# A decoder layer on one core: the last two products of the down stage share an output and its banks, the gate's dots move to the second block's map

## Chip, cores and metric

The kernel runs on 1 core of one Trainium2 chip. Times are device microseconds of one execution; the time of a kernel is the median of its runs. Engines are TensorE (PE; its weight loads are PEld), VectorE (DVE), ScalarE (ACT), GpSimd (POOL) and SyncE (SP); in this kernel SP and POOL issue the DMAs.

## The reference

Shapes: x is 1 × 2048 × 1024, the hidden width is 4096, one layer, all in float32.

```python
mod = (cond @ w_ada[l] + b_ada[l])[:, None, :]
sh1, sc1, g1, sh2, sc2, g2 = jnp.split(mod, N_MOD, axis=-1)
...
mix = jnp.concatenate([y_conv, y_pool], axis=-1) @ w_out[l]
x = _layer_norm(DEEPNORM_ALPHA * x + (1.0 + g1) * mix, ln1_g[l], ln1_b[l])

h = x * (1.0 + sc2) + sh2
f = jnp.square(jax.nn.relu(h @ w_mlp_in[l])) @ w_mlp_out[l]
x = _layer_norm(DEEPNORM_ALPHA * x + (1.0 + g2) * f, ln2_g[l], ln2_b[l])
```

The change touches the last three lines: the two products of the MLP, the gate g2 (a row of 1024 numbers, itself a product of `cond` with a part of `w_ada`) and the last normalisation.

## The kernel before

**Precision.** Each float32 operand is cut in two: ACT makes the high part by a cast (L145), the DVE the rest by a subtraction (L146, the "split"). A product of two operands is then three matmuls (L152, L153, L154: high × high, high × low, low × high), called `mm3` here.

**Stages.** The 2048 tokens are two blocks of 1024, b = 0 and 1. For each block: input projection with the token mixing, output projection with the first normalisation, then `first_map`, which makes the hidden state and squares its positive part. When both blocks are done, `down` multiplies the hidden state by w2 and normalises. In the profiled execution the stages lie about so: block 0 to 283, its map 283 to 575, block 1's input projection 575 to 745, its output projection to 845, its map 845 to 1149, down 1149 to 1717, the rest the tail.

**Fast products.** The maps use a Strassen-like scheme of seven products of blocks (`up(b, g)` for eight column groups g; 24 matmuls for each of the seven, group by group, with weights summed on the fly). `down` uses a scheme with 26 products, the table `PRODUCTS`. A row of it is (slot of the hidden state's sums, weights with signs, sign, whether the banks start anew, reads). "Reads" are (t, d, sign): the product's four banks are added to output tile group t, column half d, `F[t, d]`. A product whose row says False goes on accumulating in the banks of the product of two rows before (there are two sets of four banks, `banks[n % 2]`). One product is four units of 24 matmuls (gp = 0 to 3), one for each quarter of the inner dimension.

**State sums.** The slots of the hidden state for `down` are sums of its blocks. `sums(stage)` in `up` makes them on the DVE, 256 columns at a time, and POOL stores them to `usum` in DRAM. The sums of weights are made by accumulating DMAs from POOL (`sums_down`, into `wsum`), one each seven `mm3` where `W_BEATS` says so: 27 in block 1's input projection and 53 in its map.

**Beside the first block's map.** `first_map` calls `beside` 48 times, from the end of group 0 to the end of group 7 (beats 0 to 47, seven a group). At each beat of the first block the iterator `first_side` may begin a job: `sum_x` and `sum_first` (four and two; they load, combine and store blocks for block 1's input projection), then the eight `gate_dot`s (load 512 KB of `w_ada`, one DVE dot) and `gate_row`, which turns the dots into the row g2: a bias on the DVE (L277, the tile `mod`), a transpose on PE (L225), a way through DRAM. A job that loads begins with its DMA and is finished three beats later. Loads of the dots are in POOL's queue.

**Order.** Each engine and each DMA queue runs its instructions in the order in which they are issued; `operand(n, gp)` is issued four units ahead of the unit that uses it. Tiles come from rings: `o` has ten tiles (128 × 1024), `r` five, `w` six, `h` 28, PSUM eight banks (`ps`). A tile that is asked for while all are in use makes the asking instruction wait for the oldest one's last user.

**The end.** `LATE` is the tile group that the last product writes. `read` adds a product's banks to F; where that was the last addition to F[t, d], `finish` multiplies by g2 and adds the residual, which `residual` made beforehand and saved (`rsave`), and `Close.normalise` does the last normalisation. The last product has banks of its own; its weights are multiplied by g2 in `operand` (`if n == last`), so that its banks can be added without a gate. The rows of LATE get their statistics by `bn_stats` on the DVE (L1340), all others by squares on ACT (`stats_act`, L835).

## Time and profile before

| | |
|---|---|
| median of 3 runs | 1734.94 us (1734.08 to 1737.56) |
| the profiled execution's own time | 1733.62 us |
| its span in the trace | 1731.8 us |
| granted TensorE clock, mean | 0.994 |
| bytes moved by DMA | 461.07 MB |

The span reaches from the first to the last instruction on the core; what lies around it is 1.8 us. The profile's rows read: start, duration, engine, line, operation, output<-inputs (buffer numbers left out), shape, count, and in brackets the idle time of that engine just before and what ended it. Busy times of matmuls overlap in their pipeline, so durations of 0.39 go with starts 0.23 apart.

### The profile page before, as it was taken

The page shows a single profiled execution, that of the slowest core. Times are in us where ns is not written, and L with a number is a line of the kernel's source. Part 1 is how long each engine was busy: PE and PEld are TensorE (multiplying, and loading weights), DVE is VectorE, ACT ScalarE, POOL GpSimd, SP SyncE. Part 2 cuts the span into 40 slices and gives each one's busy share as a digit, 9 for nine tenths or more (in the row PEclk, how much of TensorE's full clock was granted, in tenths as well). Part 3 has the DMA queues.
Part 4 walks back from the last instruction along what each step waited for, and adds up shares of the span by engine and source line. Part 5 has one row for each costly group of instructions (what it writes and reads, how often), then busy time and mean ns, then how long its engine had stood idle before and what let it go on. Part 6 is the DMA issues. An engine that isn't in the chain of part 4 may idle for free.

```text
span 1731.8 us, 21979 instructions
## 1 busy us (share of the span) xinstructions
PE 1691.5 (98%) x7519; PEld 1397.7 (81%) x7519; DVE 1394.1 (81%) x2123; ACT 840.7 (49%) x1148; POOL 382.4 (22%) x695
## 2 busy tenths in 40 slices
PE   9999999999999999999999999999999999999996
PEld 8888888787887778878878888888888888888885
DVE  8897798888888776878797777685788886598999
ACT  6323358555444843445854454464544433353542
POOL 0222221345544302220245555430000000000000
PEclk9999999999999999999999999999999999999998
DMA  9998777677674767895989999888899997678672
GB/s 387 346 341 316 302 264 252 211 225 243 229 220 162 236 210 214 208 330 185 305 250 263 262 263 259 227 279 335 309 336 346 354 344 289 198 246 296 243 272 94
DMA packets 146912, 461.07 MB, mean 266 GB/s; under 512 B 20200, under 2 KB 20720, under 8 KB 146800
## 3 DMA queue, kind: packets, MB, share of 16 engines
q1 hardware_dynamic: 89728, 290.80, 47.3%
q0 software_dynamic: 57072, 168.87, 32.3%
q8 instruction: 59, 0.97, 0.2%
q14 instruction: 53, 0.43, 0.1%
HBM read 345.81 MB, written 155.72 MB: 290 GB/s over the span
## 4 chain that ended last, share of the span: by engine, by line
PE 52%; DVE 10%; DMA 4%; issue 2%; ACT 1%; POOL 0%; DVEq 0%; SPq 0%; ACTq 0%; POOLq 0%
PE ps L154 17%; PE ps L152 17%; PE ps L153 17%; DVE o L162 2%; DVE h L146 2%; DVE w L146 1%; DVE h L162 1%; DVE o L1366 1%; DVE o L1361 1%; DMA r<-gout 1%; DMA r<-wosum 1%; DMA usum<-o 1%; DVE r L162 1%; PE ps L856 0%; DMA r<-in_w 0%
## 5 line engine op out<-in xcount | busy, mean ns | idle before, releaser
L154 PE MATMUL ps<-h,w 128*128 128x512 f32 x1312 | 511.9, 391 | 12.2 <-DVE w L146 12.2
L152 PE MATMUL ps<-h,w 128*128 128x512 f32 x1312 | 511.8, 391 | 5.0 <-ACT o L1070 3.0
L153 PE MATMUL ps<-h,w 128*128 128x512 f32 x1312 | 511.8, 390 | 0.0
L152 PE MATMUL ps<-h,h 128*128 128x512 f32 (+1 forms) x1064 | 412.5, 388 | 3.5 <-ACT o L730 1.7
L153 PE MATMUL ps<-h,h 128*128 128x512 f32 (+1 forms) x1064 | 412.3, 388 | 1.0 <-DVE h L146 1.0
L154 PE MATMUL ps<-h,h 128*128 128x512 f32 (+1 forms) x1064 | 412.4, 388 | 0.0
L154 PEld LDWEIGHTS ps<-h,w 128*128 128x128 f32 x1312 | 247.2, 188 | 66.4 <-DVE w L146 15.4
L152 PEld LDWEIGHTS ps<-h,w 128*128 128x128 f32 x1312 | 246.8, 188 | 57.6 <-ACT o L1070 3.4
L153 PEld LDWEIGHTS ps<-h,w 128*128 128x128 f32 x1312 | 247.2, 188 | 51.6
L1095 POOL DMA_DIRECT2D usum<-o x416 | 226.3, 552 | 276.6 <-DVE o L162 185.5
L145 ACT CAST w<-r 128x1024 fp32r<-128x1024 f32 x156 | 164.2, 1053 | 224.6 <-PE ps L153 200.4
L145 ACT CAST h<-r 128x1024 fp32r<-128x1024 f32 (+1 forms) x144 | 144.5, 1010 | 247.2 <-PE ps L153 80.3
L146 DVE TENSOR_TENSOR w<-r,w 128x1024 fp32r<-128x1024 f32 x156 | 189.3, 1218 | 79.1 <-ACT w L145 78.5
L152 PEld LDWEIGHTS ps<-h,h 128*128 128x128 f32 x1064 | 199.7, 188 | 45.7 <-ACT o L730 2.1
L146 DVE TENSOR_TENSOR h<-r,h 128x1024 fp32r<-128x1024 f32 (+1 forms) x144 | 167.1, 1167 | 84.9 <-ACT h L145 84.8
L153 PEld LDWEIGHTS ps<-h,h 128*128 128x128 f32 x1064 | 199.8, 188 | 42.0 <-DVE h L146 1.3
L154 PEld LDWEIGHTS ps<-h,h 128*128 128x128 f32 x1064 | 199.8, 188 | 40.9
L162 DVE TENSOR_TENSOR o<-o,o 128x256 f32<-128x256 f32 (+2 forms) x458 | 199.6, 484 | 3.7 <-DMA usum<-o 1.2
L162 DVE TENSOR_TENSOR o<-o,ps 128x512 f32<-128x512 f32 x172 | 114.4, 679 | 19.9 <-PE ps L154 19.1
L145 ACT CAST h<-w 128x1024 fp32r<-128x1024 f32 x104 | 108.7, 1046 | 41.2 <-DVE w L162 36.6
L146 DVE TENSOR_TENSOR h<-w,h 128x1024 fp32r<-128x1024 f32 x104 | 126.6, 1218 | 1.9 <-ACT h L145 1.6
L162 DVE TENSOR_TENSOR r<-r,r 128x1024 f32<-128x1024 f32 x60 | 73.3, 1221 | 33.0 <-DMA r<-in_w 29.6
(166 smaller groups left out, 1415.4 us busy)
## 6 DMA issues: line engine op xcount, KB each, us to landing
usum<-o POOLq DMA_DIRECT2D x416, 128.0 KB, 5.5
r<-usum SPq DMA_DIRECT2D x104, 512.0 KB, 5.4
w<-in_w SPq DMA_DIRECT2D x80, 512.0 KB, 6.3
w<-wsum SPq DMA_DIRECT2D x68, 512.0 KB, 6.7
r<-in_w SPq DMA_DIRECT2D x60, 512.0 KB, 6.9
wsum<-in_w POOLq DMA_DIRECT2D x56, 512.0 KB, 9.3
wsum<-wsum POOLq DMA_DIRECT2D x24, 512.0 KB, 6.2
msum<-o POOLq DMA_DIRECT2D x18, 512.0 KB, 7.0
```

The source lines that it names most:

```text
L145: high = nc.scalar.copy(hi, src)
L146: return high.ins, nc.vector.tensor_tensor(lo, src, hi.bitcast(F32), op=ALU.subtract).ins
L152: nc.tensor.matmul(ps, whi, xhi, start=first, stop=False, skip_group_check=goes_on)
L153: nc.tensor.matmul(ps, whi, xlo, start=False, stop=False, skip_group_check=goes_on)
L154: done = nc.tensor.matmul(ps, wlo, xhi, start=False, stop=last, skip_group_check=goes_on)
L162: return nc.vector.tensor_tensor(out_, a, b_, op=op)
L1095: nc.gpsimd.dma_start(usum[slot, g // 2, :, b, g % 2, :], z)
L1361: nc.vector.scalar_tensor_tensor(z[:, cs], self.F[t][:, cs], mv[:, 0:1], self.rows[0][:, cs], op0=op, op1=ALU.mult)
L1366: nc.vector.scalar_tensor_tensor(z[:, cs], z[:, cs], mv[:, 6:7], self.rows[1][:, cs], op0=ALU.mult, op1=ALU.add)
```

## The change

It has four parts.

1. *The end of the down stage.* The 26 products are the same; their order, some signs and shares of banks are new. The last two (slots 10 and 18, weights w0 and w2) go to the same output (2, 0): product 24 starts new banks and reads nothing, product 25 accumulates in them (`last_product` uses `banks[(last - 1) % 2]`). LATE is 2 now, not 1. Both weights are multiplied by g2 beforehand: `residual` becomes `prepared`, a list of 16 residual jobs and 8 weight jobs (load 512 KB, two DVE instructions, store to `wsum`, which has two places more), begun at product 1, not 3. `operand` multiplies nothing any more. `Close.tail`, the rows with bn_stats, is one row only; the other three use ACT's squares.
2. *The gate's dots* move from the first block's map to the second's (`second_side`), with their loads in SP's queue, begun at beats 4, 6, 11, 13, 18, 20, 25 and 27, the row at 31. The six sums of `first_side` begin at beats 5, 11, 13, 18, 20 and 26; before, at 0, 4, 8, 12, 16 and 20.
3. *The last group's state sums* of block 0 are owed to `flush`, which is called behind the first product of the next input projection.
4. `W_BEATS`' first range ends at 200, not 232.

```diff
@@ -28,7 +28,7 @@
-W_BEATS = {*range(48, 232, 7), *range(336, 752, 7)}
+W_BEATS = {*range(48, 200, 7), *range(336, 752, 7)}
 
@@ -63,32 +63,32 @@
 )
 PRODUCTS = (
-    (10, ((0, 1),), -1, True, ()),
+    (4, ((13, 1), (14, 1)), -1, True, ((2, 0, -1),)),
     (1, ((2, 1),), 1, True, ((0, 0, -1),)),
-    (18, ((2, 1),), 1, False, ((2, 0, -1),)),
+    (6, ((1, 1), (15, -1)), -1, False, ((2, 1, 1),)),
     (5, ((12, 1),), -1, False, ((0, 1, 1), (2, 1, 1))),
...
+    (20, ((4, 1),), 1, True, ((1, 0, 1),)),
     (14, ((3, 1),), 1, False, ((3, 1, -1),)),
-    (22, ((16, 1),), 1, False, ((0, 1, 1),)),
+    (2, ((3, 1), (15, 1)), -1, True, ((0, 1, -1),)),
     (24, ((8, 1),), 1, False, ((0, 1, -1),)),
-    (19, ((4, 1), (17, 1)), 1, False, ((0, 0, -1),)),
+    (12, ((1, 1),), 1, False, ()),
     (25, ((5, 1),), 1, False, ((1, 1, -1),)),
-    (20, ((4, 1),), 1, True, ((1, 0, 1),)),
+    (17, ((3, 1),), 1, False, ((2, 1, -1),)),
+    (10, ((0, 1),), 1, True, ()),
+    (18, ((2, 1),), -1, False, ((2, 0, 1),)),
 )
 
@@ -242,7 +242,7 @@
-    wsum = tc.dram_tile([W_KEPT - 8, 4, P, T], F32, name="wsum")
+    wsum = tc.dram_tile([W_KEPT - 6, 4, P, T], F32, name="wsum")
@@ -741,6 +741,7 @@
             product(0, x_, True)
             keep(cut(values, 0), x_)
+            flush()
@@ -1057,6 +1058,13 @@
     def sum_out(g, tiles):
         sum_blocks([gout[i % 2, i // 2 * 2 + g] for i in range(4)], wosum[g], tiles)
 
+    owed = []
+
+    def flush():
+        while owed:
+            made_of, stage = owed.pop(0)
+            made_of(stage)
+
     def up(b, g, B, beside, turn):
         X, Y, Z, mark = {}, {}, {}, [None]
         order = (0, 1, 5, 4, 6, 7, 3) if g else (0, 1, 7, 4, 5, 6, 3)
@@ -1152,15 +1160,23 @@
             join(c12, Z)
             beside(mark[0])
         made(c12, 0, 1)
+        late = g == NC - 1 and b + 1 < NB
         for stage in range(2 if g else 0, 3):
-            sums(stage)
+            if late:
+                owed.append((sums, stage))
+            else:
+                sums(stage)
         product(6, X, False)
         c21 = t_o()
         for p in range(2):
             mark[0] = nc.scalar.activation(c21[:, ps[p]], X[p], AF.Relu).ins
         nc.scalar.activation(c21, c21, AF.Square)
         made(c21, 1, 0)
-        sums(3)
+        flush()
+        if late:
+            owed.append((sums, 3))
+        else:
+            sums(3)
         beside(mark[0])
 
 
@@ -1172,24 +1188,33 @@
                                     accum_op=ALU.add if kind else ALU.bypass)
                 yield
 
-    def residual(order):
+    def prepared(order, raw, g2):
         ag, ab = row(t_o(D), rows[0]), row(t_o(D), rows[1])
         nc.scalar.mul(ag, ag, ALPHA)
         nc.scalar.mul(ab, ab, ALPHA)
-        loaded, summed = [], []
-        for t in order + [None, None]:
-            if summed:
-                s, r = summed.pop()
-                nc.sync.dma_start(rsave[s], r)
+
+        def gated_weights(r):
+            for hs in halves:
+                tt(r[:, hs], r[:, hs], g2[:, halves[0]], ALU.mult)
+
+        def residual(r):
+            tt(r, r, ag, ALU.mult)
+            tt(r, r, ab, ALU.add)
+
+        jobs = [(nsave[t], rsave[t], residual) for t in order]
+        jobs += [(w2[w, gp], wsum[W_KEPT - 8 + i, gp], gated_weights) for i, w in enumerate(raw) for gp in range(4)]
+        loaded, worked = [], []
+        for job in jobs + [None, None]:
+            if worked:
+                nc.sync.dma_start(*worked.pop())
             if loaded:
-                s, r = loaded.pop()
-                tt(r, r, ag, ALU.mult)
-                tt(r, r, ab, ALU.add)
-                summed.append((s, r))
-            if t is not None:
+                (_, dst, work), r = loaded.pop()
+                work(r)
+                worked.append((dst, r))
+            if job:
                 r = t_r()
-                nc.sync.dma_start(r, nsave[t])
-                loaded.append((t, r))
+                nc.sync.dma_start(r, job[0])
+                loaded.append((job, r))
             yield
 
     def down(g2, close):
@@ -1210,6 +1235,8 @@
 
         def operand(n, gp):
             s, ws, sign = PRODUCTS[n][:3]
+            if n >= last - 1:
+                ws = ((W_KEPT + n - last + 1, 1),)
             r = t_r()
             nc.sync.dma_start(r, usum[s, gp].rearrange("p b g n -> p (b g n)"))
             qs = [t_w(F32) for _ in ws]
@@ -1218,9 +1245,6 @@
             q = qs[0]
             for more, (_, plus) in zip(qs[1:], ws[1:]):
                 tt(q, q, more, ALU.add if plus > 0 else ALU.subtract)
-            if n == last:
-                for hs in halves:
-                    tt(q[:, hs], q[:, hs], g2[:, lo_], ALU.mult)
             hi, lo = t_h(), t_h()
             if sign > 0:
                 split(r, hi, lo)
@@ -1278,9 +1302,9 @@
         def last_product(ops):
             for i, R in enumerate(rows_of(LATE)):
                 for cs in [lo_] if i < 3 else QUARTERS:
-                    ps = t_ps()[:, : cs.stop - cs.start]
+                    ps = banks[(last - 1) % 2][i][:, cs]
                     for gp in range(4):
-                        unit(ps, i, ops[gp], gp == 0, gp == 3, False, cs)
+                        unit(ps, i, ops[gp], False, gp == 3, True, cs)
                     close.add(R, cs, ps)
                     close.flush()
                     close.sums(R, cs)
@@ -1290,7 +1314,8 @@
         stream = [(n, gp) for gps in (range(3), (3,)) for n in range(2) for gp in gps]
         stream += [(n, gp) for n in range(2, last + 1) for gp in range(4)]
         ready = [operand(*x) for x in stream[:4]]
-        later = residual(sorted(range(16), key=lambda R: (ends[R % 8 // 2], R)))
+        later = prepared(sorted(range(16), key=lambda R: (min(final[R % 8 // 2, d] for d in range(2)), R)),
+                         [PRODUCTS[n][1][0][0] for n in (last - 1, last)], g2)
         for k, (n, gp) in enumerate(stream):
             if n == last:
                 break
@@ -1300,7 +1325,7 @@
             _, _, _, new, reads = PRODUCTS[n]
             if gp == 0 and new:
                 banks[n % 2] = [t_ps() for _ in range(4)]
-            if n > 2 and gp % 2 == 0:
+            if n > 0 and gp % 2 == 0:
                 next(later, None)
             for i in range(4):
                 unit(banks[n % 2][i], i, ops, new and gp == 0, gp == 3, not new)
@@ -1320,7 +1345,7 @@
             self.rows = None
             self.st = None
             t = PRODUCTS[-1][4][0][0]
-            self.tail = [8 * b + 2 * t + m for b in range(2) for m in range(2)]
+            self.tail = [8 + 2 * t + 1]
 
 
         def flush(self):
@@ -1330,11 +1355,15 @@
                 self.late = None
 
         def first_half(self, t, h):
+            if t not in self.tail:
+                return
             self.st = self.st or mk(sm, [P, P], F32, "wp", 6)[:, :60].rearrange("p (a n) -> p a n", n=6)
             self.sums(t, halves[h])
 
 
         def sums(self, t, cs):
+            if t not in self.tail:
+                return
             w = self.width(t)
             for c in range(cs.start, cs.stop, w):
                 nc.vector.bn_stats(self.st[:, 2 * self.tail.index(t) + c // w, :], self.F[t][:, c : c + w])
@@ -1395,7 +1424,7 @@
 
     def gate_dot(f):
         r = t_o(D)
-        nc.gpsimd.dma_start(r, wada[f - G1])
+        nc.sync.dma_start(r, wada[f - G1])
         yield
         dot(f, r)
 
@@ -1406,24 +1435,28 @@
         row_by_dram(g2, mod[:, G2 : G2 + KD], 1)
         gate.append(g2)
 
+    def timed(jobs):
+        due = {}
+        for beat in range(48):
+            for _ in due.pop(beat, ()):
+                pass
+            if beat in jobs:
+                next(jobs[beat])
+                due[beat + 3] = jobs[beat]
+            yield
+
     def first_side():
-        idle = lambda: iter((None,))
         sums = [sum_x(n) for n in range(4)] + [sum_first(p) for p in halves]
-        jobs = [job for x in sums for job in (x, idle(), idle(), idle())]
-        jobs += [gate_dot(f) for f in range(G2, G2 + KD)] + [gate_row()]
-        begun = []
-        for job in jobs + [idle()] * 3:
-            if len(begun) == 3:
-                for _ in begun.pop(0):
-                    pass
-            next(job, None)
-            begun.append(job)
-            yield
+        return timed(dict(zip((5, 11, 13, 18, 20, 26), sums)))
+
+    def second_side():
+        rows_ = [gate_dot(f) for f in range(G2, G2 + KD)] + [gate_row()]
+        return timed(dict(zip((4, 6, 11, 13, 18, 20, 25, 27, 31), rows_)))
 
     gate = []
 
     def first_map(b, B, back):
-        side = iter(()) if b else first_side()
+        side = second_side() if b else first_side()
         open_ = []
 
         def beside(ins):
```

**What it moves, at three places.** The first is the DVE in the first block's map, in groups 2 and 3. Rows L146 with `w` are splits of a weight that PE waits for; rows L162 with `o` of 128x512 are `sum_x`'s, those of 128x256 state sums. Before:

```order
L162 TENSOR_TENSOR o_3309<-o_3309,o_3308 128x512
L162 TENSOR_TENSOR o_3305<-o_3305 128x256
L162 TENSOR_TENSOR o_3308<-o_3309,o_3308 128x512
L162 TENSOR_TENSOR o_3309<-o_3309 128x512
...
L162 TENSOR_TENSOR o_3481<-o_3481 128x256
L146 TENSOR_TENSOR w_3595<-r_3506,w_3594 128x1024
L162 TENSOR_TENSOR o_3481<-o_3481,o_3257 128x256
L162 TENSOR_TENSOR o_3481<-o_3481 128x256
L146 TENSOR_TENSOR w_3634<-r_3589,w_3633 128x1024
L146 TENSOR_TENSOR w_3673<-r_3508,w_3672 128x1024
```

Of the change, at the same splits:

```order
L146 TENSOR_TENSOR w_3614<-r_3577,w_3613 128x1024
L162 TENSOR_TENSOR o_3461<-o_3461,o_3245 128x256
L162 TENSOR_TENSOR o_3461<-o_3461 128x256
L162 TENSOR_TENSOR o_3520<-o_3520,ps_3531 128x512
L162 TENSOR_TENSOR o_3520<-o_3520,ps_3544 128x512
L146 TENSOR_TENSOR w_3655<-r_3484,w_3654 128x1024
L162 TENSOR_TENSOR o_3407<-o_3407 128x512
L162 TENSOR_TENSOR o_3562<-o_3520 128x256
L162 TENSOR_TENSOR o_3520<-o_3520 128x256
L162 TENSOR_TENSOR o_3408<-o_3408,o_3407 128x512
L162 TENSOR_TENSOR o_3407<-o_3408,o_3407 128x512
```

Before, the wide rows share a run with the group's last state sums, ahead of three splits; now they stand behind that run and behind the split of w_3655, with few narrow rows between them.

The second is the DVE at the start of the down stage. Rows L146 and L1229 (L1253 in the change) are splits of an operand, L162 with `w` the addition of two weights, L162 with `o` the last state sums. Before, both of unit 1's splits (`h_9585`, `h_9589`) stand ahead of the run of sums:

```order
L146 TENSOR_TENSOR h_9577<-w_9570,h_9576 128x1024
L162 TENSOR_TENSOR o_9457<-o_9457,o_9305 128x256
L162 TENSOR_TENSOR o_9457<-o_9457,o_9416 128x256
L162 TENSOR_TENSOR o_9383<-o_9383,ps_9403 128x512
L1229 SCALAR_TENSOR_TENSOR h_9585<-r_9580,h_9584 128x1024
L146 TENSOR_TENSOR h_9589<-w_9582,h_9588 128x1024
L162 TENSOR_TENSOR o_9416<-o_9383,o_9416 128x256
```

Of the change:

```order
L162 TENSOR_TENSOR w_9570<-w_9570,w_9571 128x1024
L162 TENSOR_TENSOR o_9457<-o_9457,o_9305 128x256
L162 TENSOR_TENSOR o_9457<-o_9457,o_9416 128x256
L162 TENSOR_TENSOR o_9383<-o_9383,ps_9403 128x512
L146 TENSOR_TENSOR h_9580<-w_9570,h_9579 128x1024
L1253 SCALAR_TENSOR_TENSOR h_9591<-r_9583,h_9590 128x1024
L162 TENSOR_TENSOR w_9585<-w_9585,w_9586 128x1024
L162 TENSOR_TENSOR o_9416<-o_9383,o_9416 128x256
...
L146 TENSOR_TENSOR h_9595<-w_9585,h_9594 128x1024
```

The first product's weights are now added first, and unit 1's weight split (the last row) stands behind 16 sums.

The third is the DVE at the end: the last row's two additions from `ps` (128x256), and what is between them. Before:

```order
L162 TENSOR_TENSOR h_10930<-h_10930,ps_14021 128x256
L1366 SCALAR_TENSOR_TENSOR o_13970<-o_13970,mv_13971,w_12390 128x1024
L820 RECIPROCAL mv_14010<-mv_14010 128x1
L821 TENSOR_SCALAR mv_14010<-mv_14010 128x1
L1361 SCALAR_TENSOR_TENSOR o_14009<-h_10928,mv_14010,w_12388 128x1024
L1340 BN_STATS wp_13890<-h_10930 128x6
L1366 SCALAR_TENSOR_TENSOR o_14009<-o_14009,mv_14010,w_12390 128x1024
L162 TENSOR_TENSOR h_10930<-h_10930,ps_14048 128x256
```

Of the change:

```order
L1383 SCALAR_TENSOR_TENSOR h_9913,mv_13787<-h_9913,ps_13808 128x512
L1395 SCALAR_TENSOR_TENSOR o_14010<-o_14010,mv_13784,w_12814 128x1024
L834 TENSOR_SCALAR mv_13787<-mv_13787 128x1
L1390 SCALAR_TENSOR_TENSOR o_14051<-h_9913,mv_13787,w_12812 128x1024
L162 TENSOR_TENSOR h_9915<-h_9915,ps_13809 128x256
L840 TENSOR_SCALAR mv_13787<-mv_13787 128x1
L1369 BN_STATS wp_13791<-h_9915 128x6
...
L1395 SCALAR_TENSOR_TENSOR o_14051<-o_14051,mv_13787,w_12814 128x1024
L162 TENSOR_TENSOR h_9915<-h_9915,ps_13809 128x256
```

Between the last row's two additions stood two wide scalings of one row and one of the row before it; now one is left.

19 rows, old and new, of the table PRODUCTS are left out of this document.

## The prediction

> **What bounds the kernel now.** I read the page first, for the engine that sets the time.
>
> ```profile
> span 1731.8 us, 21979 instructions
> PE 1691.5 (98%) x7519; PEld 1397.7 (81%) x7519; DVE 1394.1 (81%) x2123; ACT 840.7 (49%) x1148; POOL 382.4 (22%) x695
> ```
>
> TensorE (PE) is busy for 98% of the span. The change leaves the products as many and as large as they were: 26 in the down stage, eight per group in the maps. So it can only win PE's idle time and the tail behind the last matmul: 1731.8 − 1691.5 = 40 us in all, and whatever it delays adds to them. The second view cuts the span by stage (first block's map, second block's map, down); its columns are window, length, busy time of PE, weight load, DVE, ACT and POOL, granted clock, DMA share, GB/s.
>
> ```profile
> 283.00:575.00 292.00, 282.12 (x1237) 231.58 (x1236) 242.09 (x416) 157.47 (x188) 122.05 (x228) 0.99 0.64 211
> 845.00:1140.00 295.00, 292.78 (x1306) 241.87 (x1305) 225.51 (x383) 152.30 (x184) 140.53 (x239) 1.00 0.95 258
> 1149.00:1697.00 548.00, 546.92 (x2412) 452.25 (x2410) 443.80 (x532) 250.91 (x334) 8.58 (x16) 1.00 0.83 297
> ```
>
> PE idles 9.9 us in the first block's map, 2.2 in the second's, 1.1 in the down stage. The DVE is 83%, 76% and 81% busy there: a queue that can fall behind for a group, but not over a stage. The first map has DMA room (0.64), the second hardly any (0.95). Third, PE's waits in order of time, each with its idle time and releaser:
>
> ```profile
> 336.31 0.50 PE L152 MATMUL ps<-h,w 128*128 128x512 f32 x1 [3.02 <-ACT o L1070]
> 407.18 0.50 PE L154 MATMUL ps<-h,w 128*128 128x512 f32 x1 [3.21 <-DVE w L146]
> 484.64 0.50 PE L154 MATMUL ps<-h,w 128*128 128x512 f32 x1 [0.74 <-DVE w L146]
> 525.77 0.27 PE L225 MATMUL ps<-ident,mod 128*8 128x128 f32 x1 [2.29 <-DVE mod L277]
> 526.91 0.50 PE L154 MATMUL ps<-h,w 128*128 128x512 f32 x1 [0.62 <-DVE w L146]
> 587.63 0.50 PE L152 MATMUL ps<-h,w 128*128 128x512 f32 x1 [1.28 <-ACT w L145]
> 610.23 0.79 PE L154 MATMUL ps<-h,w 128*128 128x512 f32 x1 [5.54 <-DVE w L146]
> 1695.50 0.50 PE L153 MATMUL ps<-h,h 128*128 128x512 f32 x1 [1.00 <-DVE h L146]
> 1697.23 0.73 PE L152 MATMUL ps<-h,h 128*128 128x512 f32 x2 [0.30 <-ACT h L145]
> 1716.65 0.28 PE L154 MATMUL ps<-h,h 128*128 128x256 f32 x1
> ```
>
> The first five add up to the first map's 9.9, the pair at 1695 to most of the down stage's; the last row ends at 1716.93, so 14.9 us of tail follow. The two at 587 and 610 lie in the second input projection.
>
> **The tail.** Work on the DVE sets it:
>
> ```profile
> 1691.23 0.68 DVE L162 TENSOR_TENSOR w<-w,bc 128x512 f32<-128x512 f32 x1
> 1706.52 1.27 DVE L1340 BATCH_NORM_STATS2 wp<-h 128x6 f32<-128x512 f32 x2
> 1714.46 0.63 DVE L162 TENSOR_TENSOR h<-h,ps 128x512 f32<-128x512 f32 x1
> 1720.50 1.27 DVE L1366 SCALAR_TENSOR_TENSOR o<-o,mv,w 128x1024 f32<-128x1024 f32 x1
> 1724.53 0.41 DVE L162 TENSOR_TENSOR h<-h,ps 128x256 f32<-128x256 f32 x1
> 1727.38 1.41 DVE L1366 SCALAR_TENSOR_TENSOR o<-o,mv,w 128x512 f32<-128x512 f32 x2
> ```
>
> The last addition of a bank starts at 1724.53, 7.6 us after the matmul that it needs: the DVE has a backlog. It consists of the eight multiplications of the last weights by the gate, of reads and residuals of the product before the last, and of bn_stats of four rows. After the change the first are done early (5 us fewer), product 24 reads nothing, and three of the last four rows take their squares on ACT:
>
> ```profile
> 1688.56 0.71 ACT L835 ACTIVATE tmp<-h,mv 128x512 f32<-128x512 f32 x1
> 1725.74 0.30 ACT L819 ACTIVATE mv<-mv,small 128x1 f32<-128x1 f32 x1 [2.91 <-DVE mv L829]
> 1726.98 0.29 ACT L824 ACTIVATE mv<-mv 128x1 f32<-128x1 f32 x1
> ```
>
> A row then costs the DVE one addition with a sum (0.6), two scalings (2×1.2) and small ones, some 3.6 us, against 5.4 of PE (a product's 96 matmuls at 0.227, a quarter for each row): no backlog. What is left is the third row's own chain. Its bank is complete 5.4 us before PE ends; the addition (0.6), the mean (0.2), two squares on ACT (0.71 each and reading their sums, 1.6), variance and root (2.3, an estimate: the root's small ACT instructions run from 1725.74 to 1727.27, 1.5, and the variance and its crossings add some 0.8), the scaling that the new order puts ahead of the last addition (1.2), and the last row's first half between them (0.7) make 6.6, so the last addition starts about 1.2 us after PE's end. From there the chain is that of before: 1724.53 to 1731.8 is 7.3. The tail becomes 8.5 instead of 14.9, a gain of **6.4** (4.5 if the crossings take 2 us more; 7.6 if the last addition need not wait, the upper bound). The two waits at 1695 and 1697 stand behind those multiplications (the splits of the last operands): **1.3** more.
>
> **The first block's map.** The change takes the eight gate dots and the gate row away and starts the six side sums later. The wait at 525.77 is the gate row's transpose, in PE's queue ahead of its source; it goes, and the 0.62 behind it (2.9). The dots also leave the DVE:
>
> ```profile
> L273 DVE SCALAR_TENSOR_TENSOR o<-o,o 128x1024 f32<-128x1024 f32 x8 | 9.7, 1214 | 0.0
> ```
>
> with 1.2 us each near 484, where the 0.74 can go. At 407 the splits are late:
>
> ```profile
> 397.54 0.68 DVE L162 TENSOR_TENSOR o<-o,o 128x512 f32<-128x512 f32 x1
> 398.15 0.68 DVE L162 TENSOR_TENSOR o<-o 128x512 f32<-128x512 f32 x1
> 405.92 2.35 DVE L146 TENSOR_TENSOR w<-r,w 128x1024 fp32r<-128x1024 f32 x2
> ```
>
> Four 512-wide side sums (0.6 us each between starts, 2.4) stood ahead of the two splits. In the new order they stand behind that run of sums and its splits, ahead of the next pair: 2.8 of the 3.21 (2.4, plus what the copies between them took). At 336, ACT's copy into an o tile came late, because two of the side sums' tiles were taken from the ring of ten at the group's start and three stores had to land; they are now taken after it. A wait of 3.02 had a second cost:
>
> ```profile
> 338.37 0.63 PE L153 MATMUL ps<-h,w 128*128 128x512 f32 x1
> 338.79 0.63 PE L154 MATMUL ps<-h,w 128*128 128x512 f32 x1
> 408.45 0.39 PE L153 MATMUL ps<-h,w 128*128 128x512 f32 x1
> 408.68 0.39 PE L154 MATMUL ps<-h,w 128*128 128x512 f32 x1
> ```
>
> Starts are 0.42 us apart for some eight matmuls instead of 0.23, which is 1.6 us. I leave 0.9 of the wait (one store and the DVE's queue are still ahead) and take 3.7 off. Sum 2.9 + 0.7 + 2.8 + 3.7 = 10.1; the new starts stand before other splits, so I take **9** (11.5 if the wait at 336 goes wholly and the DVE leads, 3 if all but the gate row's moves on).
>
> [...]
>
> **The second block's map.** It receives what the first lost: eight loads of 512 KB, now on SP's queue, eight dots, one row, one PE transpose.
>
> ```profile
> o<-in_wada POOLq DMA_DIRECT2D x8, 512.0 KB, 5.6
> 1080.41 1.21 DVE L146 TENSOR_TENSOR w<-r,w 128x1024 fp32r<-128x1024 f32 x1
> 342.25 1.22 DVE L162 TENSOR_TENSOR r<-r,r 128x1024 f32<-128x1024 f32 x1 [5.31 <-DMA r<-in_w]
> 1099.55 1.23 DVE L162 TENSOR_TENSOR r<-r,r 128x1024 f32<-128x1024 f32 x1 [2.92 <-DMA r<-in_w]
> ```
>
> The row's transpose needs the DVE's mod, which the new order puts just ahead of the split that ran at 1080.41; PE reaches it at about 1079.9, so it waits some **0.7** (0 to 2.3, the wait of before). The dots themselves are 9.7 us of DVE work over 150 us in which the DVE has a quarter of its time free: nothing, unless one stands before a split. The loads are 4.2 MB, 16 us of transfer at the window's 258 GB/s, in a stage whose DMA has 5% of 295 us, 15 us, to spare; the later weight beats add five accumulating stores. The last two rows show how far the block loads run behind: the DVE waits 3 to 5 us for one, and PE had operands in hand in both places. I take **1** for contention (0 to 8, half the transfers' time).
>
> **Late sums and weight beats.** The flush of the last group's sums moves no instruction: the sums were already in that place in each engine's order, behind the input projection's first product. So 587 and 610 stay; **0**. Ending the first range of weight beats 32 beats earlier moves five of 27 accumulating DMAs from the second input projection to the second map, behind the place of the 5.54 wait: **0** (a gain of 1.5 at most, should the later waits of that stage shrink).
>
> **Start of the down stage.** Product 0 was one weight; it is now w13 + w14, so eight loads instead of four and an addition before each split.
>
> ```profile
> 1148.74 0.39 PE L152 MATMUL ps<-h,h 128*128 128x512 f32 x1
> 1150.42 3.44 DVE L162 TENSOR_TENSOR o<-o,o 128x256 f32<-128x256 f32 x10
> 1154.44 1.21 DVE L1229 SCALAR_TENSOR_TENSOR h<-r,h 128x1024 fp32r<-128x1024 f32 x1
> 1191.57 1.22 DVE L162 TENSOR_TENSOR w<-w,w 128x1024 f32<-128x1024 f32 x1 [10.30 <-DMA w<-in_w]
> ```
>
> PE enters the stage at 1148.74 and wants unit 1's operands at about 1154.6. Before, its weight was split before the last sums (the run at 1150.42); now its addition is, and the split stands behind 16 sums. Those take 16 × 0.34 = 5.4 us, the two additions 1.2 each, so the split is through at about 1157 to 1157.6: **3** us of wait (0 if the sums start early, 6 if the second weight's load also comes late, as at 1191.57 where an addition waited 10.3 us for one with PE ahead of it covered). In mid-stage, gating and residual jobs use the DVE's free 104 us of 548, product by product; the new table gives the busiest run of products about 6 us of backlog against four units of 5.4 us in hand: 0.
>
> **The sum**, against the profiled execution's own 1733.6: −6.4 − 1.3 − 9 + 0.7 + 1 + 3 = −12.0, so 1721.6. The median of the runs is 1.3 above the profiled one: **1723**. The small terms' bounds together give 1716 to 1729 as this case's own range.
>
> **Rivals.** First, slower: *SP's queue in the second map.* A gate load stands in SP's queue between the block loads and waits for its o tile; what is behind it waits too. For: the o ring is ten tiles, in use by the state sums, and this is the stage without DMA room. Against: the beat waits for a mark that is old when SP reaches it, and the o tiles of a group are free by then. If four of the groups with loads in them lose what the wait at 336 cost (3.0 + 1.6), that is 18.5 us: 1741. It decides from 3.0 us per group upward (the 12 gained). [...]
>
> Second: *the first map's waits only move.* Its side sums still have 12 wide DVE instructions, which now stand before the splits of other groups; the waits at 336 and 407 come back there, and only the gate row's 2.9 is won: 6 us less, 1729. For it: the stage's 83% on the DVE. Against: where the new order has four wide ones ahead of two splits, no run of state sums stands with them.
>
> Third: *the tail stays.* If the third row's crossings cost as much as the DVE's backlog did, the 6.4 is not won: 1729 to 1730. Against: in the new order one wide scaling waits for that chain ahead of the last addition; before, five wide scalings ran between the last matmul and that addition, the one at 1720.50 among them.
>
> Fourth, better: the five accumulating DMAs less and the earlier free POOL shorten the waits at 587 and 610 (1.3 + 5.5, and 1.6 of slow clock as behind 336): 8.4 less, about 1714.
>
> **Chances.** Forecast 0.53, the queue 0.15, moving waits 0.16, the tail 0.08, better 0.08. About 0.2%, 3.5 us, is what a measurement of this kernel can tell from no change: 1731.5 to 1738.4. Faster: nearly all of the forecast (0.51), 0.11 of the moving waits, 0.05 of the tail, 0.08 = 0.75. Slower: the queue's 0.14. The same: 0.11. The range from 1712 to 1733 takes in the forecast and three of the rivals, and leaves out the queue's and a little else, under 0.2.
>
> **What would show it.** Right: no PE wait above 1 us from 283 to 575, no L225 there, the last matmul about 9 us before the span's end, a wait of 2 to 3 us in the first 10 us of the down stage, and a wait below 1 us on L225 in the second map. Wrong: block loads in the second map that land more than 5 us after PE wants them with PE waiting (the queue); waits of 3 us between 283 and 575 at other groups (moving); a last addition more than 3 us behind the last matmul (the tail); or PE waits inside the down stage, in which the jobs now begin two products earlier, which no term of mine has.

## The result, and the profile after

| | before | change |
|---|---|---|
| median of 11 runs | 1735.92 us (1734.08 to 1739.71) | 1730.22 us (1726.66 to 1733.10) |
| ratio, 95% interval | | 0.9964 (0.9954 to 0.9974) |
| span of the profiled execution | 1731.8 us | 1727.6 us |

The change makes the kernel faster by 0.36%, some 6 us. The forecast was 12. The page of the changed kernel, first lines:

```profile
span 1727.6 us, 22038 instructions
PE 1694.8 (98%) x7519; PEld 1398.3 (81%) x7519; DVE 1403.3 (81%) x2138; ACT 845.3 (49%) x1160; POOL 378.7 (22%) x687
```

By stage (first map, second map, down; columns as before: PE, weight load, DVE, ACT, POOL, clock, DMA share, GB/s):

```profile
283.00:575.00 292.00, 290.48 (x1284) 239.46 (x1282) 241.60 (x410) 169.49 (x203) 117.07 (x219) 1.00 0.62 203
836.00:1148.00 312.00, 301.00 (x1303) 244.99 (x1302) 237.66 (x406) 151.65 (x183) 146.85 (x249) 0.98 0.98 268
1148.00:1697.00 549.00, 546.04 (x2402) 451.61 (x2402) 465.44 (x567) 256.13 (x338) 8.58 (x16) 1.00 0.86 312
```

PE's idle time in the first map fell from 9.9 to 1.5 us. In the second it rose from 2.2 to 11.0. PE's waits in order of time show where:

```profile
362.20 0.50 PE L154 MATMUL ps<-h,w 128*128 128x512 f32 x1 [1.18 <-DVE w L146]
598.79 0.79 PE L154 MATMUL ps<-h,w 128*128 128x512 f32 x1 [6.20 <-DVE w L146]
853.79 0.50 PE L153 MATMUL ps<-h,w 128*128 128x512 f32 x1 [0.59 <-DVE h L146]
862.33 0.49 PE L153 MATMUL ps<-h,w 128*128 128x512 f32 x1 [0.60 <-DVE h L146]
875.12 1.19 PE L152 MATMUL ps<-h,w 128*128 128x512 f32 x2 [2.91 <-DVE o L162]
1071.46 0.50 PE L152 MATMUL ps<-h,w 128*128 128x512 f32 x1 [3.00 <-ACT o L1078]
1075.77 0.80 PE L154 MATMUL ps<-h,w 128*128 128x512 f32 x1 [3.57 <-DVE w L146]
1157.52 0.50 PE L153 MATMUL ps<-h,h 128*128 128x512 f32 x1 [2.96 <-DVE h L146]
1717.17 0.39 PE L152 MATMUL ps<-h,h 128*128 128x256 f32 x1 [0.90 <-DVE h L162]
1720.03 0.28 PE L154 MATMUL ps<-h,h 128*128 128x256 f32 x1
```

Of the old waits those at 336, 407, 485, 526, 527, 762, 767, 904, 931, 1695 and 1697 are gone; the large one of the second input projection (5.54 at 610) is there as 6.20. New are one of 1.18 at 362 in the first map, two of 0.6 at the start of the second, a pair in its seventh group, one at the start of the down stage and one in the last row. The 2.91 at 875 is an old wait that has grown. Before, the same matmul waited 0.74:

```profile
885.40 0.69 PE L152 MATMUL ps<-h,w 128*128 128x512 f32 x2 [0.74 <-DVE o L162]
```

To add them up I take, from the timeline, the time of the same matmul (counted from the start, the gate row's transposes left out) in both kernels. Negative is earlier than in the kernel before:

| place (time before) | change | e1 (dots in first map) | e3 (old beats) | e6 (no gate loads) |
|---|---|---|---|---|
| first map, early (332) | -0.1 | -0.4 | -0.3 | 0.0 |
| first map, late (571) | -11.7 | -6.3 | -11.7 | -12.2 |
| input projection, end (739) | -11.2 | -2.6 | -10.3 | -11.2 |
| second map, group 0 (865) | -15.4 | -6.8 | -10.5 | -15.7 |
| second map (888) | -8.9 | -2.3 | -6.2 | -11.1 |
| second map (1072) | -9.7 | -4.4 | -6.7 | -11.5 |
| second map (1095) | -0.7 | -4.4 | +1.9 | -9.2 |
| down (1185) | +4.2 | +1.5 | +6.9 | -4.2 |

The last matmul of the change starts 3.4 us later than before (1720.03 against 1716.65). Only the tail makes it the faster kernel: 7.6 us less from there to the span's end. All that PE had won until 865, 15.4 us, is lost by 1185.

The tail on the DVE:

```profile
1718.95 1.28 DVE L1395 SCALAR_TENSOR_TENSOR o<-o,mv,w 128x1024 f32<-128x1024 f32 x1 [1.02 <-ACT mv L825]
1720.35 0.42 DVE L162 TENSOR_TENSOR h<-h,ps 128x256 f32<-128x256 f32 x1
1723.20 1.42 DVE L1395 SCALAR_TENSOR_TENSOR o<-o,mv,w 128x512 f32<-128x512 f32 x2
```

The last addition now starts at 1720.35, as the last matmul ends (1720.31). The DVE even has an idle microsecond ahead of the scaling before it; there is no backlog left.

And the place of the pair, on the DVE:

```profile
1056.88 2.48 DVE L162 TENSOR_TENSOR r<-r,r 128x1024 f32<-128x1024 f32 x2 [4.87 <-DMA r<-in_w]
1070.47 3.43 DVE L162 TENSOR_TENSOR o<-o,o 128x256 f32<-128x256 f32 x10
1074.50 1.21 DVE L146 TENSOR_TENSOR w<-r,w 128x1024 fp32r<-128x1024 f32 x1
```

The DVE waits 4.87 us for a block load, has hardly any idle time from there on (0.17 us), reaches the group's state sums late and the split behind them later still: PE waits 3.57 us for it at 1075.77. The ACT copy that PE waited for at 1071 is on the same chain, behind an addition of the DVE. SP's queue, which issues both the block loads (L594) and the gate's (L1427), waited at its head, from 900 to 1150:

```profile
SPq L594 <- DVE w L146: 108.4, 17, 27.0
SPq L1427 <- DVE o L162: 50.3, 4, 15.3
...
SPq L1427 <- DMA usum<-o: 11.0, 5, 5.6
SPq L1427 <- ACT o L1078: 10.6, 1, 10.6
```

(sum, count, longest). For 72 us the queue stood at a gate load with block loads behind it.

The block load of the 4.87 was issued at 1048.37 and landed 8.4 us later; in e6_no_loads below, which leaves the gate loads out, the same load took 8.3 us. So it was not slow to land, it was issued late. The queue did not stand at a gate load then either: it waited 7.1 us for a split of the DVE. That split had waited for ACT's cast, and ACT for a store of state sums to land and free an o tile:

```profile
1045.56 0.59 ACT L1078 COPY o<-ps 128x512 f32<-128x512 f32 x1 [4.79 <-DMA usum<-o]
1047.12 1.22 DVE L146 TENSOR_TENSOR w<-r,w 128x1024 fp32r<-128x1024 f32 x1 [4.98 <-ACT w L145]
```

From 920 to 1140 ACT's waits of this kind add up to 11.8 us in the change, and to 0.3 in the kernel before.

### The profile page after: what moved, and what is told of

Its sections match the earlier page's. It is cut to its first block, busy times and chain, and to the rows that moved or that the text cites. A ratio compares the mean times of both kernels' runs of the same rounds, so it can differ in the third digit from the quotient of the medians.

```text
span 1727.6 us, 22038 instructions
## 1 busy us (share of the span) xinstructions
PE 1694.8 (98%) x7519; PEld 1398.3 (81%) x7519; DVE 1403.3 (81%) x2138; ACT 845.3 (49%) x1160; POOL 378.7 (22%) x687
## 4 chain that ended last, share of the span: by engine, by line
PE 58%; DVE 8%; DMA 7%; issue 6%; ACT 2%; POOL 1%; DVEq 0%; POOLq 0%; SPq 0%; ACTq 0%
PE ps L154 19%; PE ps L153 19%; PE ps L152 19%; DVE o L162 4%; DMA wsum<-in_w 3%; DVE w L146 1%; DVE h L146 1%; DMA o<-hsave 1%; DMA usum<-o 1%; DMA nsave<-o 1%; DMA r<-in_w 0%; DMA r<-winsum 0%; ACT w L145 0%; DMA w<-wsum 0%; DMA r<-in_wins 0%
## 5 line engine op out<-in xcount | busy, mean ns | idle before, releaser
L154 PE MATMUL ps<-h,w 128*128 128x512 f32 x1312 | 512.4, 391 | 11.6 <-DVE w L146 11.5
L146 DVE TENSOR_TENSOR w<-r,w 128x1024 fp32r<-128x1024 f32 x156 | 190.0, 1220 | 68.4 <-ACT w L145 67.4
L145 ACT CAST h<-r 128x1024 fp32r<-128x1024 f32 (+1 forms) x136 | 136.1, 1007 | 181.0 <-PE ps L153 71.5
L162 DVE TENSOR_TENSOR o<-o,o 128x256 f32<-128x256 f32 (+2 forms) x458 | 200.2, 485 | 10.8 <-DMA o<-hsave 6.1
L146 DVE TENSOR_TENSOR h<-r,h 128x1024 fp32r<-128x1024 f32 (+1 forms) x136 | 157.5, 1165 | 56.8 <-ACT h L145 56.6
L162 DVE TENSOR_TENSOR o<-o,ps 128x512 f32<-128x512 f32 x184 | 123.0, 681 | 40.2 <-PE ps L154 38.3
L146 DVE TENSOR_TENSOR h<-w,h 128x1024 fp32r<-128x1024 f32 x104 | 126.8, 1219 | 20.4 <-ACT h L145 20.0
L162 DVE TENSOR_TENSOR o<-o 128x256 f32<-128x256 f32 (+1 forms) x176 | 81.6, 467 | 17.2 <-ACT o L1091 8.7
```

Source lines behind the costliest of these rows:

```text
L145: high = nc.scalar.copy(hi, src)
L146: return high.ins, nc.vector.tensor_tensor(lo, src, hi.bitcast(F32), op=ALU.subtract).ins
L154: done = nc.tensor.matmul(ps, wlo, xhi, start=False, stop=last, skip_group_check=goes_on)
L162: return nc.vector.tensor_tensor(out_, a, b_, op=op)
```

## Experiments

Each is the changed kernel with one edit unless said otherwise. Ratios are to the kernel before on the same chip; the map's length is from the first matmul of the second map to the first of the down stage in the profiled execution (before 311.3, change 326.0).

| run | ratio, 95% interval | second map, us |
|---|---|---|
| change | 0.9964 (0.9954 to 0.9974) | 326.0 |
| e1_dots_back | 0.9963 (0.9947 to 0.9979) | 313.7 |
| e2_pool_queue | 1.0009 (0.9997 to 1.0021) | 333.2 |
| e3_old_beats | 0.9959 (0.9945 to 0.9973) | 323.7 |
| e5_product1_first | 0.9997 (0.9987 to 1.0006) | 325.0 |
| e6_no_loads | 0.9918 (0.9897 to 0.9938) | 317.8 |
| e7_no_dots | 0.9955 (0.9939 to 0.9970) | 325.7 |
| e8_down_alone | 0.9976 (0.9958 to 0.9993) | 310.8 |
| e9_early_beats | 0.9995 (0.9982 to 1.0009) | 328.8 |
| e11_cond_kept | 0.9976 (0.9962 to 0.9989) | 313.5 |
| e12_first_map_spread | 0.9950 (0.9934 to 0.9966) | 314.2 |
| e13_small_loads | 0.9958 (0.9941 to 0.9974) | 320.9 |
| e14_bytes_alone | 0.9991 (0.9981 to 1.0001) | 331.7 |
| e15_dots_between_sums | 0.9946 (0.9931 to 0.9962) | 313.9 |
| e16_loads_unheld | 0.9973 (0.9963 to 0.9984) | 328.7 |

**The dots back in the first map.**

```diff
-    side = second_side() if b else first_side()
+    side = iter(()) if b else first_side()
...
-        return timed(dict(zip((5, 11, 13, 18, 20, 26), sums)))
+        return timed(dict(zip((5, 11, 13, 18, 20, 26, 24, 25, 27, 28, 29, 30, 31, 32, 33), sums + rows_)))
...
-        nc.sync.dma_start(r, wada[f - G1])
+        nc.gpsimd.dma_start(r, wada[f - G1])
```

> The change, but the eight gate dots and the gate row stand beside the first block's map again, their loads in POOL's queue; all else as changed (median 1730.2, profiled span 1727.6). In the changed kernel the second block's map has 17.5 us beyond 0.227 us a matmul, 8.8 of it around 1071 to 1080. Theory A (the gate loads wait in SP's queue for o tiles, up to 15.3 us at 50.3 us in four waits, and hold the block loads behind them): those 8.8 us go, the first block's map pays 2 to 4 again; the time falls by 5 to 7, to 1723 to 1725. Theory B (the 4.2 MB are too much for a stage at a DMA share of 1.0): the same. Theory C (what is won ahead of the second map is waited for in it whatever it holds): the excess of the second map stays above 13 us and the time rises by the 2 to 4, to 1732 to 1734.

The pair at 1071 is gone. One wait is left in the second map, at its start (881.72): it is the matmul that waits 2.91 at 875 in the change.

```profile
PE ps L152 <- DVE o L162: 3.9, 1, 3.9
```

The map is 12.3 us shorter. But the first map and the next input projection are 8.6 longer, where theories A and B had allowed 2 to 4, and the time stays. So the move of the dots, for which the forecast had 1.9 us (2.9 and 0.7 won, against 0.7 and 1), is worth nothing that the times show. Theory C in its strong form falls: the second map does lose less when it holds less.

**The loads from POOL's queue.**

```diff
-        nc.sync.dma_start(r, wada[f - G1])
+        nc.gpsimd.dma_start(r, wada[f - G1])
```

> The change, but the gate dots' loads in the second block's map are issued from POOL's queue; bytes, beats and dots are the same. Theory A (SP's queue): the pair of waits around 1071 (3.0 and 3.6 us with slow clock, 8.8 in all) goes or shrinks below 2; the time falls by 6 to 9, to 1721 to 1724. Theory B (bytes): block loads are as late as in the changed kernel, the pair stays, time within 2 us of 1730. Theory C: the excess of the second map stays, elsewhere.

The pair stays (3.0 and 3.1) and four waits of over 1 us come up between 943 and 1042. The DVE now waits for the gate loads themselves, 28.4 us in four waits, the one ahead of the pair:

```profile
1061.41 1.23 DVE L273 SCALAR_TENSOR_TENSOR o<-o,o 128x1024 f32<-128x1024 f32 x1 [7.00 <-DMA o<-in_wada]
```

The pair does not need SP's queue: here a gate load that is late where the DVE wants it, in order, makes it. By the ratio the time is some 8 us above the change's, which no theory had.

**The old weight beats.**

```diff
-W_BEATS = {*range(48, 200, 7), *range(336, 752, 7)}
+W_BEATS = {*range(48, 232, 7), *range(336, 752, 7)}
```

> The change, but the first range of weight beats ends at 232 again (five accumulating DMAs go back from the second map to block 1's input projection). If the beats made the waits of 1.5 and 1.7 us at 762 and 767 of the kernel before: they come back, 3.7 us longer until the second map begins. Theory C then says that the second map's first 45 us give most of it back (their 6.4 us of waits shrink): 1728 to 1732. If the start of the second map is late for another reason: its waits stay and the time is 1733 to 1735. If the beats had nothing to do with 762 and 767: no change, 1730.

The waits ahead of the second map are there again:

```profile
751.56 0.50 PE L152 MATMUL ps<-h,h 128*128 128x512 f32 x1 [1.54 <-DVE o L162]
756.29 0.50 PE L152 MATMUL ps<-h,h 128*128 128x512 f32 x1 [1.70 <-ACT o L730]
```

So the beats made them, which the prediction had put at 0. By the ratio the new beats gain nothing: by 888 the second map has given 4.3 us back (-10.5 to -6.2 in the table), where the change gives 6.5, and the ratio is the change's. Across the runs, what is won before group 0 is partly lost in it: of 15.4 us 6.5, of 10.5 4.3, of e1's 6.8 4.5; e8_down_alone, which comes 2.0 us late, loses 0.4. The DVE waits there for loads of hsave (4.75 us at 849 in the change). This is a relation over several runs, not an experiment on its cause.

**Product 1 first.**

```diff
-        stream = [(n, gp) for gps in (range(3), (3,)) for n in range(2) for gp in gps]
+        stream = [(n, gp) for gps in (range(3), (3,)) for n in (1, 0) for gp in gps]
```

> The change, but the down stage begins with product 1's units (one weight each) ahead of product 0's (two weights). My theory (the wait of 2.96 us at 1157.5 is the addition of two weights, with the split behind 16 state sums): the wait falls below 0.5 and the time by 2.5 to 3, to 1727. Rival (the DVE's queue at the stage's start is late anyhow; product 0's additions wait three units later in the same way): a wait of 1 to 3 us appears within the first 35 us of the stage and the time stays within 1 us of 1730.

The wait at 1157 is gone, as my theory said. But 1.27 and 0.77 come one unit later, at 1161, as the rival said, and then another:

```profile
1202.16 0.80 PE L152 MATMUL ps<-h,h 128*128 128x512 f32 x1 [6.73 <-ACT h L1270]
```

PE waits for ACT's copy of a bank into F. The time rises by 6 us; neither theory had that. That the two weights make the wait of 2.96 agrees with e8_down_alone below, where it is 2.48 with all maps as before.

**No gate loads.**

```diff
     def gate_dot(f):
-        r = t_o(D)
-        nc.sync.dma_start(r, wada[f - G1])
         yield
-        dot(f, r)
+        r = t_o(D)
+        nc.vector.scalar_tensor_tensor(r, cond, 1.0, cond, op0=ALU.mult, op1=ALU.mult,
+                                       accum_out=acc[:, f : f + 1])
```

> The change without the eight loads of the gate's weights in the second block's map: each dot multiplies the row cond by itself (so g2 is not the reference's), with the same DVE instruction, o tile, beat and row. Theory L (the loads in SP's queue and in the DMA engines make a block load late, the DVE waits 4.9 us for it at 1056.9 of the changed kernel and hands that on to PE as 3.0 + 3.6 at 1071 and 1076): the DVE's wait falls to 3 or less and the pair goes; the second map's excess falls from 17.5 to about 8, the time by 7 to 9 against the change, ratio about 0.9920. Theory D (the dots' DVE work and the row): pair and time stay, ratio 0.996.

Theory L, as forecast: the pair shrinks to one wait.

```profile
1068.96 0.50 PE L154 MATMUL ps<-h,w 128*128 128x512 f32 x1 [1.85 <-DVE w L146]
```

The ratio falls by 0.46 of a percent, 8 us, with the dots' DVE work in place. The run takes three things away at once: the bytes, the queue's waits at these loads, and the time for which each load holds an o tile.

**No dots.**

```diff
-        dot(f, r)
+        nc.vector.tensor_copy(acc[:, f : f + 1], cond[:, f : f + 1])
```

> The change with the eight loads in SP's queue, but without the dots: in place of each dot a copy of one column that does not wait for the load (so g2 is not the reference's). Theory L: block loads are as late as in the changed kernel, the pair of waits around 1071 stays, ratio 0.996. Theory D (9.7 us of dots on the DVE): the pair goes, ratio 0.991 to 0.992. The start of the second map (waits of 0.6, 0.6 and 2.9 between 853 and 876) is ahead of the first dot; neither theory changes it.

```profile
1068.86 0.50 PE L152 MATMUL ps<-h,w 128*128 128x512 f32 x1 [1.03 <-ACT o L1078]
1073.60 0.79 PE L154 MATMUL ps<-h,w 128*128 128x512 f32 x1 [4.00 <-DVE w L146]
```

The pair stays and so does the time. The dots on the DVE cost nothing that can be measured; the loads cost 8 us.

**The first part alone** (the side sums, the dots and the beats of the kernel before in the changed kernel).

> The kernel before with the first part of the change alone (order of products, shared banks, weights gated ahead, statistics on ACT; the late sums, which move nothing, are in it too). If the parts add up: tail 7.6 shorter, down stage 4.1 longer, maps as before: 3.5 us less, ratio 0.998. If the late start of the down stage (2.96) comes from the second map's lateness and not from the two weights: 6 to 7 us less, ratio 0.996.

4.2 us less by the ratio, two thirds of the whole gain. The interval takes in both forecasts; the profiled execution decides. From the last matmul to the end it takes 7.5 us, as the change does, and the wait at the start of the down stage is there (2.48 at 1159) though the second map is as long as before (310.8): the parts add up.

**The row cond kept.** The dots' other operand, `cond`, is one of the ten o tiles, and it is in use until the last dot; the change so leaves nine for block 1. On e1_dots_back:

```diff
+    def hold():
+        for beat in range(48):
+            if beat == 30:
+                nc.vector.tensor_copy(acc[:, 0:1], cond[:, 0:1])
+            yield
...
-        side = iter(()) if b else first_side()
+        side = hold() if b else first_side()
```

> e1_dots_back (dots in the first map) with one small read of the row cond, which lies in one of the ten o tiles, at beat 30 of the second block's map, so that nine tiles are left until there as in the change. Theory R (the tile that cond holds is what makes the second map's start late): the DVE's wait for the first load of hsave grows from 0.3 to 4 or 5 us and the waits of 0.6 at 18 and 26 us of the map come back as in the change; the time rises by 1 to 4 us, ratio 0.997 to 0.9985. If the tile is not missed: same waits and ratio as e1_dots_back, 0.9963.

The DVE's wait for the first load of hsave came back (0.26 in e1, here as below), and with it two small waits (0.18 and 0.61), but the map's length is the same (313.5): the tile is not what makes the map's start cost time. The 3.0 us by which the profiled execution falls behind e1's are lost by 523, in the first map. The ratio lies in theory R's range, but the intervals of the two ratios overlap: a cost of 0 to 3 us, not settled.

```profile
859.81 1.22 DVE L162 TENSOR_TENSOR o<-o,o 128x1024 f32<-128x1024 f32 x1 [3.46 <-DMA o<-hsave]
```

**Small loads, bytes without a tile, loads not held, early beats.** Four runs on whether the bytes or the queue's wait make the block loads late.

```diff
 # e13, on e7
-        nc.sync.dma_start(r, wada[f - G1])
+        nc.sync.dma_start(r[:, :8], wada[f - G1, :, :8])
```

> e7_no_dots with each of the eight loads cut to 8 of its 1024 columns (32 bytes a row instead of 4 KB, so g2 is not the reference's): SP's queue still waits for the o tile of each load (46 us in four waits and 21 in five in e7_no_dots) and holds the block loads behind it, but 4.2 MB no longer move. Theory A (the wait at the head of SP's queue is what makes the block loads late): the pair of waits around 1069 to 1074 (1.0 and 4.0 us) and the DVE's wait of 4.9 or more for r<-in_w stay, second map 324 to 326 us, ratio 0.9955. Theory B (the bytes, in a stage at a DMA share of 1.0): they go as in e6_no_loads, second map 317 to 319 us, ratio 0.992.

```diff
 # e14, on e7
-        r = t_o(D)
-        nc.sync.dma_start(r, wada[f - G1])
+        nc.sync.dma_start(copied[f - G2], wada[f - G1])
```

> e7_no_dots with the eight loads going to DRAM, not to an o tile: the same 4.2 MB are read (and written) at the same beats from SP's queue, but no load waits there for an o tile. The dots are left out (so g2 is not the reference's). Theory A (the wait at the head of SP's queue): the block loads are in time, the waits around 1069 to 1074 fall below 2.7, second map 318 us or less, ratio 0.992. Theory B (bytes): the waits stay at 4 us or more, second map 324 to 326, ratio 0.9955 or higher.

```diff
 # e16
-            if open_:
+            if open_ and b:
+                next(side, None)
+            elif open_:
                 with behind(ins):
                     next(side, None)
```

> The change with the second map's side jobs no longer tied behind the beat's mark (an instruction of ACT or the DVE that each of their DMAs waits for): the eight gate loads stand at nearly the same places of SP's queue and wait for their o tile alone; the same bytes move, all dots are done. In the change SP waits 72 us at the head of its queue for these loads. Theory A (that wait is what makes block loads late): SP's wait at the gate loads falls below 20 us, the pair of 3.0 and 3.6 us around 1071 goes, second map 318 to 320 us, ratio 0.992 to 0.993. Theory B (bytes): the pair, or waits of the same sum in other groups, stay; second map 324 to 328, ratio 0.996 to 0.998. If SP's wait does not fall, the o tile makes it, and A against B stays open.

```diff
 # e9
-        return timed(dict(zip((4, 6, 11, 13, 18, 20, 25, 27, 31), rows_)))
+        return timed(dict(zip((4, 6, 8, 11, 13, 15, 18, 20, 24), rows_)))
```

> The change with the second map's jobs begun at beats 4, 6, 8, 11, 13, 15, 18 and 20, the row at 24: no gate load in groups 5 and 6. Where a load at the wrong beat makes one block load late (theory A or B alike), the pair around 1071 goes, since the two loads ahead of it (beats 25 and 27) have gone; if groups 1 to 3 have room for two more loads the time falls by 6 to 8, ratio 0.992. If the stage is short of bytes as a whole, waits of 1 to 3 us come up in groups 2 to 4 instead and the time stays within 2 us, ratio 0.995 to 0.997.

e13 (wait without bytes) came out between: the profiled execution's map is 4.8 us shorter than e7's, with one wait of 2.53 left at this place, but its ratio is e7's: without the bytes no time was won. e14 didn't make its case: SP still waited 80 us for the beats' marks, and the copies write as many bytes again. In e16 SP's wait at the gate loads fell from 72 to 32 us, not below 20, and the pair at 1071 went; in its place came, among others, these, and the map is longer:

```profile
922.33 0.79 PE L152 MATMUL ps<-h,w 128*128 128x512 f32 x1 [2.32 <-ACT w L145]
1042.75 0.50 PE L154 MATMUL ps<-h,w 128*128 128x512 f32 x1 [1.55 <-DVE w L146]
1133.92 0.79 PE L152 MATMUL ps<-h,w 128*128 128x512 f32 x1 [2.34 <-ACT o L1078]
```

e9 is alike: nothing at 1071, but 5.11 at 989 and 2.93 at 1042. So an earlier beat or a shorter wait only moves the lost time to other groups while the loads stay in the stage; without them (e6) or with the dots elsewhere (e1, e12, e15) it goes. Whether it is the bytes, the queue's wait or the o tile that each load holds isn't shown: e13's profile speaks for the bytes and its ratio against them, and no run takes the tiles alone away. ACT's waits for a store to free an o tile (920 to 1140) bear on it. They are 11.8 us in the change, 10.1 in e7, 7.4 in e3, 7.3 in e9 and 6.6 in e5, and at most 1.1 in all other runs: they come where loads of full size wait in SP's queue for the beat's mark and take an o tile. In e9 two of them, of 3.88 at 969 and 3.45 at 1017, stand 20 to 24 us ahead of PE's waits at 989 and 1042, much as the 4.79 does in the change. They are not the only way to lose the time: e2, e14 and e16 have hardly any and are no faster.

**The dots in the first map, spread.** Two orders, both with loads in SP's queue and no second side.

```diff
 # e12
+        return timed(dict(zip((5, 11, 13, 18, 20, 26, 28, 30, 32, 34, 36, 38, 40, 42, 44), sums + rows_)))
 # e15
+        return timed(dict(zip((5, 11, 13, 18, 20, 26, 8, 15, 22, 24, 28, 30, 32, 34, 38), sums + rows_)))
```

> The change with the dots and the row beside the first map, where the DMA share is 0.62, in SP's queue, but behind the side sums and one every two beats (28 to 42, row at 44), not one a beat as in e1_dots_back (24 to 33), where an o tile that a store still held made ACT wait 4.3 us at 509. If the crowding was what the first map paid 9 us for: its waits at 515 and 518 go, at most 3 us stay, the second map stays at 314 and the time falls by 6, ratio 0.992 to 0.993. If the first map's last groups have no room for the dots' tiles at any spacing: waits of 2 to 4 us in groups 5 to 7 and ratio 0.996.

> The change with the dots beside the first map between the side sums (beats 8, 15, 22, 24, 28, 30, 32, 34, the row at 38), loads in SP's queue. In e12_first_map_spread (28 to 42, row at 44) PE had lost nothing against the change until 571 us and then 8.8 us in the first 40 us of the next input projection, where the last dots and the row fall. If the dots' late end is what costs: those 8.8 us stay won, the second map stays at 314 us, the time is 7 to 9 below the change, 1721 to 1723, ratio 0.991 to 0.992. If the DVE has no room for dots earlier in the map: waits of 2 to 4 us between 400 and 575 and ratio 0.995 to 0.997.

e12 lost nothing until 571 and then 8.8 us in the input projection. In e15 the dots stand earlier, and the loss comes earlier too: waits of 1.74, 2.52 and 1.82 on a split at 441, 482 and 522, one for each group. Both have the second map at 314, as they should. Their ratios, 0.9950 and 0.9946, are the best of the kernels that compute the reference, but their intervals overlap the change's; neither is shown to beat it. The dots cost some 9 us in the first map's neighbourhood or 12 and more in the second map, at every place that was tried.

## Why the prediction came half true

- **The tail**: right. -6.4 was said, -7.6 measured. The last addition doesn't wait for the third row's chain; the upper bound of that term was the truth. The two waits at 1695 and 1697 went, as said; a wait of 0.90 that I hadn't seen came at 1717: the last row's two quarters now share a bank, and PE waits until the DVE has read the first (its addition runs from 1716.70 to 1717.11).
- **The first block's map**: right. -9 was said, with 11.5 as a bound; it is -11.6 between 332 and 571, the bound again. The waits at 336 and 407 went for good. The sign of being right, "no PE wait above 1 us from 283 to 575", failed by one wait of 1.18 at 362. The second rival, that the waits would only move, is out.
- **Late sums**: the waits at 587 and 610 stayed, as said (0.87 and 6.20 now); no run tests the sums alone. **Weight beats**: "0 (a gain of 1.5 at most)" failed. They removed 762 and 767, 4.2 us from 739 to 865. Some half of it is given back in the next 25 us (e3 against the change).
- **The second block's map** is the step that failed. "I take 1 for contention (0 to 8)" plus 0.7 for the row; it is 14.7 us longer (326.0 against 311.3), more than the 8 that I had set as the bound. Some 8 of these are the gate loads (e6 against the change), the transpose none (L225 has no wait at 1078.07). The rest lies at the map's start, after an arrival 15.4 us earlier, which my sum let count in full; why an earlier arrival is lost there stays open. I had one warning in numbers: 16 us of transfer for 15 us of free DMA time. The 1 rested on the DVE's waits of 3 to 5 us that had cost PE nothing. They had cost nothing at 342 and 1099; at 1056 a wait of 4.87, with the state sums behind it, cost 6.6 and a granted clock of 0.52 from 1075.7 to 1079.7. And no term of mine had the ten o tiles: ACT waited for one (11.8 us in the change), and that made the block load late.
- **The first rival** named the place and the sign, not the time (1741). "The beat waits for a mark that is old when SP reaches it" was wrong: SP stood 72 us at these loads. And "the o tiles of a group are free by then" was wrong too: without the marks SP still stood 32 us there (e16). But its price of four groups with 4.6 each was one group with 9.0, the block load that was late there was not held by a gate load, and taking more than half the wait away (e16) didn't bring the time back.
- **The start of the down stage**: right in its wait, 2.96 for a predicted 3; with the slow clock behind it (0.57 from 1157.5 to 1161.5) 4.9. I had priced such a clock in the first map (1.6 behind the wait at 336, where it was 0.65 from 336.3 to 341.2) and left it out here.

In sum: won 11.6 + 4.2 + 7.6 and 0.8 at the end of the down stage, lost 14.7 (6.5 at the start, 9.0 at the pair, with 0.8 won between), 0.5 in the input projection and 4.9, with 0.1 from before 332 on the winning side: -4.2 in the profiled execution. The terms were said to give -12.

That the time still lies between 1712 and 1733 is in part luck: two terms came out at their upper bounds and one that was put at 0 gave 4.2, and these set off a loss beyond its bound. Nor did "1716 to 1729" follow from the terms' bounds: all at their best or all at their worst, they give 1713 and 1742.

## What to carry to other kernels

Eight loads of 512 KB, moved into a stage with a DMA share of 0.95, cost 8 us here, though the transfers (16 us, an estimate from 4.2 MB at the stage's 258 GB/s) were hardly longer than the free DMA time (15 us) and the engine that reads them, the DVE, had a quarter of its time free (busy for 225.5 of 295 us before). Before such a move, ask for more than the bytes: what the loads stand before in their queue, and which tiles they hold that others wait for. These runs don't settle which of the three it was. Time that is won ahead of such a stage isn't won until the stage's end has been seen to move. And a wait of the DVE's that cost nothing in one group (2.92 us at 1099, before) cost PE nearly twice its length in another (4.87 us of the DVE at 1056, 9.0 of PE), where a run of other work stood between it and what PE wanted next.

## What the runs showed of the hardware

The slow clock after a wait isn't tied to the wait's length alone. In the change the waits of 2.91 (875) and 2.96 (1157) were followed by some six and some eight matmuls 0.43 us apart instead of 0.23; the granted clock was 0.50 there (875.1 to 878.1) and 0.57 (1157.5 to 1161.5):

```profile
1158.56 0.63 PE L153 MATMUL ps<-h,h 128*128 128x512 f32 x1
1158.98 0.63 PE L154 MATMUL ps<-h,h 128*128 128x512 f32 x1
```

In e15 a wait of 2.00 (at 579) was followed by matmuls 0.43 us apart too. In the kernel before, the wait of 3.02 (at 336) had a granted clock of 0.65 behind it (336.3 to 341.2), the longer one of 3.21 (at 407) one of 1.00 (407.2 to 411.2). What decides between the two these rows do not show.
